# A planner that models a shared port between VectorE and GpSimd, in a fused hybrid-mixer and mixture-of-experts kernel

## The chip, the cores and the metric

The kernel runs on one core of a Trainium2 chip. A core has five engines that each work through their own instruction queue in order: TensorE (PE in the profile; its weight loads are the row PEld), VectorE (DVE), ScalarE (ACT), GpSimd (POOL) and SyncE (SP, which here issues nearly all transfers). They meet only at semaphores. The metric is the device time of one execution in microseconds (us), lower is better. Before the change the median of three runs is 1183.54 us.

## What is computed

One decoder layer over 1024 tokens of width 1024, in f32: a mixer with three kinds of causal heads, and a mixture of 32 experts of which each token uses two.

```python
h = rmsnorm(x, norm_mix) * (1.0 + scale_m) + shift_m          # scale, shift, gate from c @ w_ada
proj = h @ w_in                                               # 13 column blocks
o_ret  = retention_chunkwise(rope(rq), rope(rk), rv)          # fixed decay per head
o_hgrn = gated_linear_recurrence_chunkwise(q, k, hi, log_f)   # gate per key dimension
o_gla  = gated_linear_recurrence_chunkwise(gq, gk, gv, log_a)
merged = concat(headnorm(o_ret) * silu(rg), headnorm(o_hgrn) * silu(hg), headnorm(o_gla) * silu(gg))
x = x + gate_m * (merged @ w_out)
h = rmsnorm(x, norm_ffn) * (1.0 + scale_f) + shift_f
out = sum over the token's 2 experts of weight * ((silu(h @ w_gate[e]) * (h @ w_up[e])) @ w_down[e])
return rmsnorm(x + gate_f * out, norm_final)
```

## The kernel before

**Tiling and stages.** The tokens are eight tiles of 128, worked on in two halves of four. Each half goes through the input projection (`tok_chunk`, `t_chunk`), the retention heads (`ret_gen`), and then the gated recurrence of the HGRN2 and GLA heads together. That recurrence is the part with the most vector work: for each token tile, `hg_prep1` makes decay-weighted queries and keys at six levels (64, 32, 16, 8, 4, 2), a base level and a carried state; `hg_gen` multiplies them on TensorE, `hg_merge` writes the masked products into one score tile, `hg_dec` multiplies by the values and `hg_state` updates the carried state. Between the halves and behind the second one the output projection (`ev_out`), the second norm (`ffn_gen`) and the router (`router`) run tile by tile. Last come the 32 experts (`gate_up_gen`, `down_gen`), which stream about 100 MB of expert weights.

**Weights in two halves.** f32 weights are multiplied as two parts in the faster matmul format: `split_gen` casts a weight granule (`raw`) to a high part (`wg`, part 0) and `split_lo` subtracts that from the original to get the low part. A `raw` buffer, of which there are two, is free for the next load only when its low part is made. The normalised tokens (`HT`) are split in the same way in `spread_ev`.

**What sets the order.** The kernel is written as Python generators that a planner (`Sched`) runs when the program is built. Each engine is an `Eng` object with a planned time `free` at which its last instruction ends. Every emitted instruction goes through `Eng.__getattr__`, which prices it with `Eng.cost` and tells `Sched.note`; `note` puts its start at the later of the engine's `free` and the end of what it depends on. A generator yields until a planned time or condition, so the planned times decide in which order instructions of different generators enter each engine's queue, and when a buffer counts as free. On the chip no planned time exists: the queues run in order, and waits are semaphores.

**Choice of engine.** Two helpers choose by planned times. `av` copies on ScalarE or VectorE. `vg` takes a two-operand operation and puts it on VectorE (`V`) or GpSimd (`G`), whichever is planned to end sooner:

```python
tv = max(V.free, d) + 0.068 + 0.00104 * n + bias
tg = max(G.free, d) + 0.13 + 0.00214 * n
```

Here `n` is the number of elements per partition and `d` the time at which the inputs are there. `vg` is used for the low part of the weights (with a bias against VectorE), most of the level preparation in `hg_prep1`, the rotary sum in `ev_rope`, the gate products and head norms, the residual sum in `ev_out` and the shift in `ffn_gen`. Both engines are planned as if they never hindered each other. Nearly all rows of the profile carry line 216, the helper through which every operation is recorded, so rows are told apart by their tiles: `rx` is the recurrence's workspace, `qkc` holds queries, keys and cumulated gates, `Zh` the carried state, `om`/`oh` mixer outputs, `tmp` a scratch of 384 columns, `h`, `x` and `B` the second norm's output, input and shift.

Of the kernel before, what the change touches and what calls it, by code (L numbers as in the profile page):

```python
# [80 lines left out]
class Sched:  # L81
# [3 lines left out]
    def __init__(self):  # L85
        self.t, self.h, self.n = 0.0, [], 0
        self.base = self.end = self.last = 0.0
        self.le = None
        self.dma_free = 1.7

    def add(self, gen, delay=0.0):
        self._push(self.t + delay, gen, None)
# [38 lines left out]
    def dep(self, e):  # L131
        return self.last + (LAT if self.le is not None and self.le is not e else 0.0)

    def note(self, e, c, n=0):
        st = max(e.free, self.dep(e))
        if e.kind == "pe":
            k = int(st / WARM)
            if e.win.get(k - 1, 0.0) < 0.41 * WARM:
                c *= 2
            if n > 1:  # L140
                e.win[k] = e.win.get(k, 0.0) + min(c, (k + 1) * WARM - st)
                if st + c > (k + 1) * WARM:
                    e.win[k + 1] = st + c - (k + 1) * WARM
        e.free = self.last = st + c
        e.busy += c
        self.le = e
        self.end = max(self.end, e.free)
# [7 lines left out]
def _size(ap):  # L155
    n = 1
    for s in ap.shape[1:]:
        n *= s
    return n


class Eng:
    def __init__(self, sch, eng, kind, is_psum):
        self.sch, self.eng, self.kind, self.is_psum = sch, eng, kind, is_psum
        self.free = self.busy = 0.0
        self.win = {}
        self.table = None

# [43 lines left out]
    def __getattr__(self, name):  # L212
        f = getattr(self.eng, name)

        def call(*a, **k):
            r = f(*a, **k)  # L216
            if a:
                small = self.kind != "pe" and _size(a[0]) < 64
                self.sch.note(self, self.cost(name, a, k) + (0.12 if small else 0.0), _size(a[0]))
            return r  # L220
        return call

# [45 lines left out]
def build(tc, A, CB, CM, coff, out):  # L268
# [6 lines left out]

    V = Eng(sch, nc.vector, "dve", is_psum)
    G = Eng(sch, nc.gpsimd, "pool", is_psum)
    T_ = Eng(sch, nc.tensor, "pe", is_psum)
    SC = Eng(sch, nc.scalar, "act", is_psum)

# [13 lines left out]
    def tt(e, o, a, b, op):  # L294
        return e.tensor_tensor(o, a, b, op=op)

    def vg(o, a, b, op, bias=0.0):
        n = _size(o)
        d = sch.last + LAT
        tv = max(V.free, d) + 0.068 + 0.00104 * n + bias  # L300
        tg = max(G.free, d) + 0.13 + 0.00214 * n
        return tt(V if tv <= tg else G, o, a, b, op)

    def ts(e, o, a, s1, op0, s2=None, op1=None):
        if op1 is None:
            return e.tensor_scalar(o, a, s1, None, op0=op0)
        return e.tensor_scalar(o, a, s1, s2, op0=op0, op1=op1)
# [7 lines left out]
    def mm(o, l, r, start, stop):  # L315
        return T_.matmul(o, l, r, start=start, stop=stop, skip_group_check=True)

# [127 lines left out]
    def rstd_of(dst, ss, n, width):  # L445
        ts(G, dst, ss, 1.0 / n, OP.mult, EPS, OP.add)
        tt(G, dst, dst, epsc[:, 0:1].to_broadcast([P, width]), OP.pow)

# [4 lines left out]
    def start_gen():  # L453
# [4 lines left out]
        def wload(i):  # L458
            c = (i % 2) * D + (i // 2) * 256
            src = w_ada[:, c:c + 256].rearrange("(k p) n -> p k n", p=P)  # L460
            for h in range(2):
                ks = slice(4 * h, 4 * h + 4)
                w_at[i, h] = dma(slots[i % 4][:, ks], src[:, ks, :])
# [14 lines left out]
        wload(3)  # L478
        G.memset(epsc[:, 0:1], -0.5)
        G.memset(Zr, 0.0)  # L480
        G.memset(Zh, 0.0)
        yield (max(p_at, c_at),)
        prow = yield from mss.take()
        T_.transpose(prow[:, 0:32], rv_[0:32], ident[0:32, 0:32])
        yield None
# [104 lines left out]
    def consts_gen():  # L590
# [4 lines left out]
        prow = yield from mss.take()  # L595
        T_.transpose(prow[:, 0:NROW - 32], rv_[32:NROW], ident[32:NROW, 32:NROW])
        yield None
# [37 lines left out]
    def spread_g(g, dst_slot, src_of, scale, bias, key):  # L635
        pt = yield from mss.take()
        pv = pt.rearrange("p (k c) -> p k c", k=2)
        for kk in range(2):
            for j in range(2):
                T_.transpose(pv[:, kk, j * P:(j + 1) * P],  # L640
                             src_of(j)[:, (2 * g + kk) * P:(2 * g + kk + 1) * P], ident)
        add(spread_ev(pt, pv, g, dst_slot, scale, bias, key), max(0.0, T_.free - sch.t) + LAT)
        yield None

    def spread_ev(pt, pv, g, dst_slot, scale, bias, key):
        if key[0] == "h" and ("AB", g) not in done:
            yield lambda: ("AB", g) in done
        h32 = yield from h32s.take()
        for kk in range(2):
            k = 2 * g + kk  # L650
            if bias is None:
                act(h32[:, kk], pv[:, kk], AF.Copy, scale=scale[:, k:k + 1])
            else:
                act(h32[:, kk], pv[:, kk], AF.Identity, scale=scale[:, k:k + 1], bias=bias[:, k:k + 1])
        mss.put(pt)
        yield None
        hv = HS[dst_slot][:, 0, 2 * g:2 * g + 2]
        if key[0] == "h" and key[1] in HVG:
            av(hv, h32)
            vg(HS[dst_slot][:, 1, 2 * g:2 * g + 2], h32, hv.bitcast(F32), OP.subtract, HBIAS)  # L660
        else:
            V.tensor_copy(hv, h32)
            tt(V, HS[dst_slot][:, 1, 2 * g:2 * g + 2], h32, hv.bitcast(F32), OP.subtract)
        h32s.put(h32)
        done.add(key + (g,))
# [102 lines left out]
    def split_lo(i, w, raw, n):  # L768
        vg(w[:, 1, :, 0:n], raw[:, :, 0:n], w[:, 0, :, 0:n].bitcast(F32), OP.subtract, LO_BIAS if ("AB", 3) in done else LO_BIAS + SBIAS)
        raws.put(raw)  # L770
        w_ready[i] = (w, sch.end + LAT)
        yield 0.0
# [28 lines left out]
    def tok_chunk(first, n, groups, slots, hkey, ev, hook=None):  # L801
        for gi_, grp in enumerate(groups):
            acc = {}
            for g in range(4):
                yield from w_wait(first + g)
                for t in grp:
# [19 lines left out]
                    if g == 3:  # L826
                        add(ev(t)(p), T_.free + LAT - sch.t)
                    yield (T_.free - LEAD,)
# [55 lines left out]
    def ev_rope(t, which):  # L884
        def f(p):
            if "trig" not in done:
                yield lambda: "trig" in done
            if t >= 4 and not which:
                yield lambda: ("st", {4: 1, 5: 2, 6: 3, 7: 3}[t]) in done
            dst = RQK[:, t % 4, which, :]  # L890
            t2 = yield from t384.take()
            pv = p[:, 0:384].rearrange("p (h f) -> p h f", f=32)
            tt(V, dst.rearrange("p (h f) -> p h f", f=32), pv,
               cosT[:, t, None, :].to_broadcast([P, 12, 32]), OP.mult)
            ph = p[:, 0:384].rearrange("p (h two f) -> p h two f", two=2, f=32)
            th = t2.rearrange("p (h two f) -> p h two f", two=2, f=32)
            sb = sinT[:, t, None, :].to_broadcast([P, 6, 32])
            stt(th[:, :, 0, :], ph[:, :, 1, :], -1.0, sb, OP.mult, OP.mult)
            tt(V, th[:, :, 1, :], ph[:, :, 0, :], sb, OP.mult)
            mput(p)  # L900
            yield None
            vg(dst, dst, t2, OP.add)
            t384.put(t2)
            yield None
            d3 = dst.rearrange("p (h c) -> p h c", h=6)
            vg(d3, d3, cc("gk" if which else "gq")[:, :, None].to_broadcast([P, 6, 64]), OP.mult)
            done.add(("rope", which, t))
        return f
# [1365 lines left out]
```

## Time and profile before

| what | us |
|---|---|
| runs of the kernel before (three) | 1183.54 median, 1182.93 to 1193.45 |
| the profiled execution itself | 1184.01 |
| its span in the trace | 1182.2 |
| VectorE busy | 841.3 (71%), 1402 instructions |
| GpSimd busy | 419.9 (36%), 424 instructions |

A row of the profile names the engine, the operation, the tile that it writes and those that it reads (`out<-in`), the size as partitions x elements, and, in a list of groups, how often it occurs, its busy time, the mean duration of one, and the idle time of the engine just before such instructions. A row of the timeline gives start, duration, the instruction, and in brackets the idle time before it with what ended it. The chain of waits is followed back from the last instruction to whatever released each one. The profiled execution took 1.8 us more than its span.

### The profile page before, as it was taken

How to read it: one execution, taken by the hardware profiler on the slowest of the kernel's cores; microseconds unless marked ns; L12 is line 12 of the kernel's file. 1: busy time of each engine (PE TensorE's matmuls, PEld its weight loads, DVE VectorE, ACT ScalarE, POOL GpSimd, SP SyncE). 2: the span in 40 equal slices, each digit the busy share in tenths (PEclk: the TensorE clock that was granted, in tenths of full speed). 3: DMA queues.
4: the chain of work that ended last, by engine and by line, in shares of the span. 5: the costliest groups of instructions: out<-in, count | busy, mean ns of one | idle time of the engine just before them, and what ended most of it. 6: DMA issues, size and time to landing. Idle time of an engine off the chain costs nothing.

```text
span 1182.2 us, 17072 instructions
## 1 busy us (share of the span) xinstructions
PE 1042.8 (88%) x6168; PEld 853.1 (72%) x6168; DVE 841.3 (71%) x1402; ACT 520.3 (44%) x974; POOL 419.9 (36%) x424
## 2 busy tenths in 40 slices
PE   3889999888989889997899999849999898899995
PEld 2889998787878788897888888736566555455654
DVE  6685767988897754448798976658666666565767
ACT  4513334455543423345455545336445444344544
POOL 4452232445633422104463413351322323332225
PEclk9889999799999999998899989859999999999997
DMA  9475556111213522233421158865999999999976
GB/s 313 140 213 185 163 167 219 41 54 31 96 54 123 172 77 58 60 92 111 137 77 41 41 177 308 302 216 155 303 295 311 302 318 307 294 315 318 329 232 261
DMA packets 96039, 218.99 MB, mean 185 GB/s; under 512 B 13342, under 2 KB 56538, under 8 KB 95954
## 3 DMA queue, kind: packets, MB, share of 16 engines
q1 hardware_dynamic: 89010, 201.67, 51.5%
q0 software_dynamic: 6944, 16.22, 6.1%
q8 instruction: 50, 0.82, 0.3%
q14 instruction: 35, 0.29, 0.1%
HBM read 201.64 MB, written 24.38 MB: 191 GB/s over the span
## 4 chain that ended last, share of the span: by engine, by line
PE 38%; DMA 25%; DVE 21%; issue 6%; ACT 4%; POOL 4%; SPq 0%; DVEq 0%; POOLq 0%; ACTq 0%; another core or an unknown queue 0%
PE mm L216 25%; DMA HG<-expert_w_up 10%; PE lv L216 10%; DVE rx L216 5%; PE ms L216 4%; DMA gu<-expert_w_up 4%; DMA dn<-expert_w_down 3%; DVE qkc L216 3%; DMA dg<-expert_w_down 3%; DMA h<-w_ada 2%; DVE HT L216 2%; DVE wg L216 2%; DMA raw<-w_in 2%; DVE h L216 1%; DVE tmp L216 1%
## 5 line engine op out<-in xcount | busy, mean ns | idle before, releaser
L216 PE MATMUL mm<-wg,HT 128*128 128x384 f32 (+2 forms) x1920 | 365.5, 343 | 24.3 <-DVE tmp L216 14.2
L216 PEld LDWEIGHTS mm<-wg,HT 128*128 128x128 f32 x1920 | 322.5, 199 | 36.6 <-issue 12.3
L216 PE MATMUL mm<-ew,xT 128*96 128x512 f32 x576 | 166.9, 428 | 10.2 <-DVE ew L216 8.0
L216 ACT ACTIVATE wg<-raw 128x768 fp32r<-128x768 f32 (+2 forms) x115 | 89.3, 779 | 124.3 <-PE mm L216 73.9
L216 PEld LDWEIGHTS mm<-ew,xT 128*96 128x96 f32 x576 | 92.4, 167 | 63.1 <-issue 15.2
L216 POOL TENSOR_TENSOR wg<-raw,wg 128x768 fp32r<-128x768 f32 (+1 forms) x36 | 69.8, 1942 | 188.8 <-ACT wg L216 119.6
L216 DVE TENSOR_TENSOR wg<-raw,wg 128x768 fp32r<-128x768 f32 (+2 forms) x90 | 83.6, 930 | 65.3 <-ACT wg L216 64.6
L216 PE MATMUL lv<-rx 64*128 64x64 f32 (+5 forms) x1216 | 104.8, 287 | 18.3 <-DVE rx L216 14.0
L216 POOL DMA_INDIRECT x2d<-y,tki x30 | 60.1, 2004 | 166.5 <-DVE y L216 74.9
L216 PEld LDWEIGHTS lv<-rx 64*128 64x128 f32 (+2 forms) x1216 | 92.9, 192 | 35.8 <-issue 22.6
L216 DVE TENSOR_TENSOR ew<-HG,ew 128x1024 fp32r<-128x1024 f32 x68 | 81.7, 1219 | 33.7 <-ACT ew L216 33.7
L216 PE MATMUL mm<-HT,wg 128*128 128x256 f32 (+1 forms) x576 | 97.6, 324 | 0.1
L216 ACT ACTIVATE rx<-rx 128x64 f32<-128x64 f32 (+4 forms) x180 | 68.6, 417 | 52.1 <-DVE rx L216 30.2
L216 ACT ACTIVATE ew<-HG 128x1024 fp32r<-128x1024 f32 x66 | 68.3, 1052 | 50.9 <-DMA HG<-expert_w_up 45.0
L216 PEld LDWEIGHTS mm<-HT,wg 128*128 128x128 f32 x576 | 82.3, 190 | 9.0 <-issue 1.0
L216 POOL DMA_INDIRECT xg<-h2d,tki x32 | 43.5, 1359 | 94.6 <-PE ms L216 74.6
L216 DVE SCALAR_TENSOR_TENSOR y<-lv,lists,GF 96x512 f32<-96x512 f32 x64 | 45.0, 741 | 44.1 <-PE lv L216 44.1
L216 PE MATMUL mm<-ewx,xT 128*96 128x512 f32 x192 | 60.7, 449 | 5.3 <-DVE ewx L216 4.5
L216 PE MATMUL lv<-dn,hT 128*96 128x512 f32 x128 | 60.8, 597 | 1.7 <-ACT hT L216 1.7
L216 PE MATMUL lv<-dg,hT 128*96 128x512 f32 x128 | 60.0, 594 | 2.3 <-ACT hT L216 2.3
L216 DVE TENSOR_TENSOR rx<-rx,qkc 128x320 f32<-128x320 f32 (+4 forms) x94 | 58.6, 652 | 1.1 <-ACT rx L216 1.0
L216 POOL TENSOR_TENSOR rx<-qkc 128x512 f32<-128x512 f32 (+2 forms) x34 | 36.0, 1066 | 45.4 <-PE lv L216 40.6
(307 smaller groups left out, 1706.3 us busy)
## 6 DMA issues: line engine op xcount, KB each, us to landing
raw<-w_in SPq DMA_DIRECT2D x64, 384.0 KB
HG<-expert_w_gate SPq DMA_DIRECT2D x46, 512.0 KB
HG<-expert_w_up SPq DMA_DIRECT2D x46, 512.0 KB
h<-w_ada SPq DMA_DIRECT2D x32, 512.0 KB
dn<-expert_w_down SPq DMA_DIRECT2D x32, 512.0 KB
dg<-expert_w_down SPq DMA_DIRECT2D x32, 512.0 KB
raw<-w_out SPq DMA_DIRECT2D x26, 384.0 KB
gu<-expert_w_gate SPq DMA_DIRECT2D x18, 512.0 KB
```

The lines of the kernel that those rows point to most:

```text
L216: r = f(*a, **k)
```

## The change

`Eng` gets two new fields: `held`, the planned end of the last operation of this engine that uses a port common to VectorE and GpSimd, and `other`, which links the two engines. An operation on one of them counts as using the port when it writes at least 64 elements per partition, is no memset, and either has more than one SBUF operand or touches no PSUM at all. `note` then starts it no sooner than the other engine's `held`, and sets its own. `vg` adds the other engine's `held` to both estimates. No operation is added or removed, and no other rule of the planner is touched.

```diff
-    def note(self, e, c, n=0):
+    def note(self, e, c, n=0, port=None):
         st = max(e.free, self.dep(e))
+        if port is not None:
+            st = max(st, port.held)
+            e.held = st + c
...
-        self.free = self.busy = 0.0
+        self.free = self.busy = self.held = 0.0
+        self.other = None
...
                 small = self.kind != "pe" and _size(a[0]) < 64
-                self.sch.note(self, self.cost(name, a, k) + (0.12 if small else 0.0), _size(a[0]))
+                port = None
+                if self.other is not None and _size(a[0]) >= 64 and name != "memset" and (
+                        sum(hasattr(x, "shape") and not self.is_psum(x) and _size(x) > 1 for x in a[1:]) > 1
+                        or not any(self.is_psum(x) for x in a if hasattr(x, "shape"))):
+                    port = self.other
+                self.sch.note(self, self.cost(name, a, k) + (0.12 if small else 0.0), _size(a[0]), port)
...
+    V.other, G.other = G, V
...
-        tv = max(V.free, d) + 0.068 + 0.00104 * n + bias
-        tg = max(G.free, d) + 0.13 + 0.00214 * n
+        tv = max(V.free, d, G.held) + 0.068 + 0.00104 * n + bias
+        tg = max(G.free, d, V.held) + 0.13 + 0.00214 * n
```

The program that comes out has 347 instructions in GpSimd's order where there were 441, and 1511 in VectorE's where there were 1426; ScalarE's go from 941 to 950. By kind, what left GpSimd are 19 low parts of weights (13 of 768 columns, 6 of 512), 9 level subtractions `rx<-qkc` of 512 columns, some 20 level products `rx<-rx,qkc`, and gate products, head norms, residual sums and shifts. All engines' orders are rearranged around that. The helper's line number becomes 220.

GpSimd's queue at the last output projection, ahead of the router: `om`, `x` and `h` with numbers are the residual and the second norm of tiles 4 and 5, `rs` the norm's factor, `wg` a weight's low part. Before:

```order
L216 TENSOR_TENSOR wg_6553<-raw_6462,wg_6553 128x2x256
L216 TENSOR_TENSOR om_6483<-om_6483,tmp_6693 128x256
L216 TENSOR_TENSOR x_6493<-x_6493,tmp_6706 128x256
L216 TENSOR_SCALAR rs_6726<-ss_6725 128x1
L216 TENSOR_TENSOR rs_6726<-rs_6726,epsc 128x1
L216 TENSOR_SCALAR rs_6740<-ss_6739 128x1
L216 TENSOR_TENSOR rs_6740<-rs_6740,epsc 128x1
L216 TENSOR_TENSOR om_6487<-om_6487,B_126 128x512
L216 TENSOR_TENSOR h_6497<-h_6497,B_126 128x512
L216 TENSOR_TENSOR wg_6779<-raw_6683,wg_6779 128x768
L216 TENSOR_SCALAR r_gm<-r_m_6789 128x1
```

And after, on the same engine at the same place:

```order
L220 TENSOR_TENSOR wg_6384<-raw_6301,wg_6384 128x768
L220 TENSOR_SCALAR rsh<-ssh 128x10
L220 TENSOR_TENSOR rsh<-rsh,epsc 128x10
L220 TENSOR_SCALAR rs_6726<-ss_6725 128x1
L220 TENSOR_TENSOR rs_6726<-rs_6726,epsc 128x1
L220 TENSOR_SCALAR rs_6749<-ss_6748 128x1
L220 TENSOR_TENSOR rs_6749<-rs_6749,epsc 128x1
L220 TENSOR_SCALAR r_gm<-r_m_6779 128x1
```

The two residual sums, the two shifts and the low parts have left GpSimd's queue here; only the norm factors and the router's small operations stay.

VectorE's queue in the recurrence of the first half, from the head norm (`ssh`) of its first tile to the first update of the carried state `Zh`. Before:

```order
L216 CAST wg_2236<-raw_2044 128x768
L216 TENSOR_REDUCE ssh<-lv_2227 128x6
L216 TENSOR_REDUCE ssh<-lv_2227 128x4
L216 TENSOR_TENSOR rx<-qkc 128x512
L216 TENSOR_TENSOR Zh<-Zh,rx 128x384
L216 TENSOR_TENSOR Zh<-Zh,rx 128x256
L216 TENSOR_TENSOR rx<-qkc 128x512
L216 TENSOR_TENSOR rx<-rx,qkc 128x16x16
L216 TENSOR_TENSOR rx<-rx,qkc 128x20x16
L216 CAST wg_2286<-raw_2220 128x768
L216 TENSOR_TENSOR rx<-rx,qkc 128x32x8
L216 TENSOR_TENSOR rx<-rx,qkc 128x40x8
```

And after, on the same engine at the same place:

```order
L220 TENSOR_TENSOR wg_2214<-raw_2065,wg_2214 128x768
L220 TENSOR_REDUCE ssh<-lv_2238 128x6
L220 TENSOR_REDUCE ssh<-lv_2238 128x4
L220 TENSOR_TENSOR Zh<-Zh,rx 128x384
L220 TENSOR_TENSOR Zh<-Zh,rx 128x256
L220 TENSOR_TENSOR wg_2266<-raw_2219,wg_2266 128x768
L220 TENSOR_TENSOR Zh<-Zh,lv_2251 64x3x64 x2
L220 TENSOR_TENSOR Zh<-Zh,lv_2251 32x64 x4
L220 TENSOR_TENSOR rx<-qkc 128x512 x2
L220 TENSOR_TENSOR rx<-rx,qkc 128x16x16
L220 TENSOR_TENSOR rx<-rx,qkc 128x20x16
```

The two casts of high parts have gone to ScalarE and two low parts have come from GpSimd, and the state update stands ahead of the next tile's level work instead of behind it.

## The prediction

> **What bounds the kernel now.** I read the page's busy shares and its chain of waits first, then the stages, then VectorE and GpSimd side by side, then their groups.
>
> ```profile
> PE 1042.8 (88%) x6168; PEld 853.1 (72%) x6168; DVE 841.3 (71%) x1402; ACT 520.3 (44%) x974; POOL 419.9 (36%) x424
> PE 38%; DMA 25%; DVE 21%; issue 6%; ACT 4%; POOL 4%; SPq 0%; DVEq 0%; POOLq 0%; ACTq 0%; another core or an unknown queue 0%
> ```
>
> TensorE leads the chain, VectorE has a fifth of it, GpSimd a twenty-fifth. The stages differ (columns: stretch in us, its length, busy time and count of PE, PEld, DVE, ACT, POOL, granted clock, DMA share, GB/s):
>
> ```profile
> 0.00:95.00 95.00, 66.58 (x325) 63.20 (x326) 69.56 (x145) 36.33 (x57) 45.76 (x52) 0.91 0.69 220
> 95.00:207.00 112.00, 108.66 (x836) 101.40 (x834) 75.16 (x92) 41.22 (x67) 27.81 (x22) 1.00 0.58 182
> 207.00:390.00 183.00, 161.00 (x1206) 147.07 (x1206) 156.54 (x267) 88.55 (x203) 83.99 (x74) 0.94 0.22 69
> 390.00:532.00 142.00, 133.61 (x838) 120.75 (x837) 79.56 (x155) 51.08 (x94) 34.15 (x45) 0.99 0.32 90
> 532.00:715.00 183.00, 166.31 (x1226) 153.24 (x1226) 155.00 (x293) 92.61 (x216) 80.39 (x90) 0.92 0.33 106
> 715.00:787.00 72.00, 51.46 (x337) 48.73 (x336) 45.46 (x140) 26.73 (x63) 29.89 (x57) 0.82 0.78 270
> 787.00:1182.00 395.00, 355.14 (x1412) 218.73 (x1412) 260.05 (x314) 183.73 (x277) 117.89 (x87) 0.96 0.89 287
> ```
>
> The third and fifth rows are the two recurrences; the second and fourth are mostly projections, with TensorE at 97% and 94%. TensorE is busy 88% and 91% there, VectorE 86% and 85%: they pace each other, and TensorE's idle 22.0 and 16.7 us bound what faster vector work can win. The last row, the experts, has DMA at 0.89 and hardly an operation that the planner may move; I expect it to shift as a block.
>
> Now the two engines at one place of the first recurrence, VectorE first:
>
> ```profile
> 249.17 0.68 DVE L216 TENSOR_TENSOR rx<-qkc 128x512 f32<-128x512 f32 x1
> 249.77 0.81 DVE L216 TENSOR_TENSOR rx<-rx,qkc 128x256 f32<-128x256 f32 x2
> 250.98 3.29 DVE L216 TENSOR_TENSOR rx<-rx,qkc 128x256 f32<-128x256 f32 x2
> ```
>
> ```profile
> 248.59 2.51 POOL L216 TENSOR_TENSOR rsh<-rsh,epsc 128x10 f32<-128x10 f32 x1
> 250.69 1.27 POOL L216 TENSOR_TENSOR rx<-qkc 128x512 f32<-128x512 f32 x1
> 251.92 2.00 POOL L216 TENSOR_TENSOR wg<-raw,wg 128x768 fp32r<-128x768 f32 x1
> ```
>
> The same pair of level products takes 0.81 us and, beside two large GpSimd operations, 3.29. Lost: 2.48 us of 3.27 us of GpSimd time, 0.76 per us. The small power `rsh` beside the first two rows costs them nothing. So the port that the change models exists, and only GpSimd's large operations hold it. The Trainium skill's page "SBUF — State Buffer" (Who interferes with whom) says that a VectorE instruction with two SBUF inputs and a GpSimd one that reads SBUF exclude each other, the later waiting for the other's end; the pair at 250.98 agrees, the power does not.
>
> How much of this there is, by VectorE's groups (busy, mean ns of one), with an undisturbed row for their forms, the last of them with the shortest of the scans as first of three durations:
>
> ```profile
> L216 DVE TENSOR_TENSOR wg<-raw,wg 128x768 fp32r<-128x768 f32 x61 | 62.2, 1021 | 41.9 <-ACT wg L216 41.6
> L216 DVE TENSOR_TENSOR rx<-qkc 128x512 f32<-128x512 f32 x32 | 27.4, 862 | 1.9 <-PE lv L216 1.8
> L216 DVE TENSOR_TENSOR rx<-rx,qkc 128x320 f32<-128x320 f32 x42 | 25.9, 620 | 0.5 <-ACT rx L216 0.5
> L216 DVE TENSOR_TENSOR HT<-h,HT 128x512 fp32r<-128x512 f32 x24 | 24.8, 1032 | 5.2 <-ACT HT L216 4.5
> L216 DVE TENSOR_TENSOR_SCAN qkc<-cst,qkc 128x128 f32<-128x128 f32 x32 | 23.1, 784 | 0.1
> L216 DVE SCALAR_TENSOR_TENSOR h<-x,rs,A 128x512 f32<-128x512 f32 x12 | 17.4, 1452 | 1.4 <-POOL rs L216 1.4
> L216 DVE TENSOR_TENSOR rx<-rx,qkc 128x256 f32<-128x256 f32 x25 | 13.5, 540 | 0.5 <-ACT rx L216 0.5
> ...
> 726.89 0.95 DVE L216 TENSOR_TENSOR wg<-rw,wg 128x768 fp32r<-128x768 f32 x1
> 218.66 0.47 DVE L216 TENSOR_TENSOR rx<-rx,qkc 128x320 f32<-128x320 f32 x1
> 325.72 0.69 DVE L216 TENSOR_TENSOR HT<-h,HT 128x512 fp32r<-128x512 f32 x1
> 730.80 0.75 DVE L216 SCALAR_TENSOR_TENSOR om<-om,rs,A 128x512 f32<-128x512 f32 x1 [0.22 <-POOL rs L216]
> L216 DVE TENSOR_TENSOR_SCAN qkc<-cst,qkc x32: 391/418/2027, 207.4 to 546.9; 128x128 f32<-128x128 f32 x32
> ```
>
> Mean less undisturbed, times count: wg 4.3, rx 512 5.8, rx 320 6.3, HT 8.2, scans 12.6, h 8.4, rx 256 3.4 (at half of 0.81): 49.0 us lost in seven groups.
>
> **The change, part by part.** Nothing is computed less; operations change engine. GpSimd's groups before:
>
> ```profile
> L216 POOL TENSOR_TENSOR wg<-raw,wg 128x768 fp32r<-128x768 f32 x29 | 58.9, 2033 | 122.9 <-DVE wg L216 67.9 <-ACT wg L216 53.7 <-DMA h<-w_ada 0.7
> L216 POOL TENSOR_TENSOR rx<-qkc 128x512 f32<-128x512 f32 x24 | 29.1, 1218 | 42.8 <-PE lv L216 38.3 <-DVE qkc L216 4.5
> L216 POOL TENSOR_TENSOR rx<-rx,qkc 128x256 f32<-128x256 f32 x23 | 21.3, 929 | 18.2 <-ACT rx L216 18.2
> L216 POOL TENSOR_TENSOR rx<-rx,tmp 128x384 f32<-128x384 f32 x10 | 13.8, 1384 | 20.7 <-DVE tmp L216 18.2 <-DVE r_ne L216 1.8 <-DVE r_m L216 0.7
> L216 POOL TENSOR_TENSOR wg<-raw,wg 128x512 fp32r<-128x512 f32 x7 | 10.9, 1565 | 65.9 <-ACT wg L216 65.9
> L216 POOL TENSOR_TENSOR om<-om,tmp 128x384 f32<-128x384 f32 x8 | 8.9, 1116 | 13.8 <-DVE tmp L216 13.8
> L216 POOL TENSOR_TENSOR h<-h,B 128x512 f32<-128x512 f32 x5 | 8.0, 1599 | 3.6 <-DVE h L216 3.6
> ```
>
> *The exchange.* By the orders, these leave GpSimd for VectorE: 13 wg of 768 columns, 9 rx of 512, 14 rx of 256, 7 rx of 384, 6 wg of 512, 7 om, 4 h. Off GpSimd: 26.4 + 11.0 + 13.0 + 9.7 + 9.4 + 7.8 + 6.4 = 83.7 us. Onto VectorE, at 0.95, 0.68, 0.41, 0.55, 0.69, 0.55, 0.69 (0.55 lies between the rows for 320 and 512 columns): 12.4 + 6.1 + 5.7 + 3.9 + 4.1 + 3.9 + 2.8 = 38.9 us. So VectorE wins only if each us that GpSimd holds the port costs it more than 38.9 / 83.7 = 0.46 us. These are 60 of the 94 that GpSimd's order has less; the rest have the same sizes or smaller ones, and I let them trade alike, so that GpSimd loses some 110 us in all and VectorE gains some 50 of its own work. A further gain or loss lies in where the moved operation stands: on GpSimd it ran beside VectorE and had a short queue; on VectorE it ends in half the time once it starts, but starts behind all that VectorE was given before it.
>
> *What a held us costs.* From below: the seven VectorE groups lose 49.0 us against 150.9 us of the seven GpSimd groups, 0.32. From above: the pair's 0.76. I take 0.4: it is a mean that is wanted, so the group figure is nearer, raised because VectorE's smaller groups also lose. Both ends stay for the range. At 0.4 VectorE gets back 33.5 of its 38.9 us: nearly an even trade.
>
> *The recurrences.* From the first scan of a half to its fourth state update VectorE's order grows by 25 and 33 instructions. They are nearly all of the forms without wg: 41 such moved ones take 47.9 us off GpSimd and put 22.4 on VectorE, 1.17 and 0.55 each. So +13.8 and +18.2 on VectorE, 29.3 and 38.6 off GpSimd, at 0.4 giving back 11.7 and 15.4: +2.1 and +2.8, about +5. With VectorE at 85% I charge all of it to the path; whatever waits next is TensorE for `rx`. Queued behind a moved operation are the masked writes of the scores and the state update, and TensorE's next level or value product waits for those.
>
> *The output projections and the second norm.* Here the path runs through these operations:
>
> ```profile
> PE mm L216 <- DVE tmp L216: 18.7, 11, 4.4
> PE ms L216 <- POOL x L216: 2.5, 1, 2.5
> 727.06 1.38 POOL om L216
> 728.45 1.41 POOL x L216
> ```
>
> The 18.7 us of TensorE wait on a product that stands in VectorE's queue behind the `h` operations, which are stretched from 0.75 to 1.45. Four of five `h<-h,B` leave GpSimd, so I strike four fifths of their 8.4 us, -6.7, and add 4 x 0.69 = 2.8. The two residual sums of 256 columns in the chain cost 2.79 us on GpSimd and some 0.42 each on VectorE: -1.9. Sum -6.
>
> *Weights.* A low part that ends sooner frees `raw` sooner, and the chain runs through that:
>
> ```profile
> 159.08 1.31 POOL wg L216
> 160.40 4.96 DMA raw<-w_in
> ```
>
> The 512-column low parts of this stage leave GpSimd and take 0.69 us in place of 1.31, two such places in the chain, and about 0.9 more for a 768-column one: -2. The price is a longer line on VectorE: before its 61 wg of 768 columns it sits idle 41.9 us, 0.69 each, for ScalarE's cast, so 19 more bring some 13 us in which what stands behind them waits too. In the projections its idle 36.8 and 62.4 us cover that. In the recurrences the cover is thin; what falls there I leave to the lower end of the exchange.
>
> *The start.* Three `HT` low parts move to VectorE in front of its matrix-vector sums: +2.1, against about as much lost now to the same operations on GpSimd. Zero, with +-3 for the range. On SyncE's queue two raw loads move ahead of the mask's load, and the mask is needed only in the recurrence, over 100 us later.
>
> *The experts.* Their order holds the same instructions, and the transfers at 0.89 cover them. Zero; if a buffer freed elsewhere let the expert loads begin at another time, that is the last row's 395 us moving, which I count as wrong below.
>
> Sum: +5 - 6 - 2 = -3, and -4 with the two casts of 768 columns that go from VectorE to ScalarE, whose 88.6 and 92.6 busy us of 183 cover them. The profiled execution took 1184.0 (0.5 over the median): **1180 us**, its own range 1172 to 1190.
>
> **Rivals.** *The block is nearly whole.* The mechanism of the pair at 250.98, everywhere: VectorE's next two-operand operation waits until GpSimd's has ended. At 0.76 the recurrences get back 51.6 for 32.0: -20, and with the other two terms 1184 - 28 = 1156. It fits inside TensorE's 38.7 idle us. For it: scans and HT take twice and one and a half times their undisturbed rows. Against it: the groups' mean is under half of the pair's, since much of the time VectorE has something to do, or to wait for, that the port doesn't touch. By the rule of the Trainium skill's page named above, one us lost for each held, the recurrences would win 35.9 and the sum would be an estimated 1140; the group means don't agree with it as an average.
>
> *VectorE's queue becomes the bound.* Place: the two recurrences. The moved operations cost 32.0 us, but what stretches VectorE is mostly the GpSimd work that stays (18 low parts and 15 of 24 level subtractions), so little comes back. At 0.1 per us 6.8 comes back: +25 - 8, 1201. It ends over 1% slower once the exchange pays under 0.18. For it: VectorE at 85% while GpSimd stands at 45%, and the planner now charges GpSimd for VectorE's whole planned queue. Against it: the 0.32.
>
> *It doesn't do what it says:* the orders change, but the loss just moves to other pairs: 1184.
>
> **How the numbers follow.** Forecast 0.40, whole block 0.27, VectorE bound 0.25, nothing 0.08. Within 1% (about what a measurement of this kernel can tell from no change) means 1171.7 to 1195.4. Faster: 0.27 and 0.04 of the forecast's low end, 0.31. Slower: 0.25. Same: 0.44. The range 1157 to 1203 leaves out half of the whole-block case and a quarter of the VectorE case, 0.20.
>
> **What would show it.** Right: the groups' means on VectorE fall toward 0.68, 0.95, 0.41 with about half of the excess gone; VectorE's busy time stays within 15 us of 841; GpSimd's falls by about 100; TensorE's wait for `tmp` falls by 4 to 8; the recurrences last 183 +-6 each. Wrong: a recurrence that shrinks by 10 (whole block) or grows by 10 with PE waiting for `rx` (VectorE bound), or a change in the experts' 395 us.

## The result and the profile after

| kernel | runs | median us | range |
|---|---|---|---|
| before, on the same chip | 4 | 1184.97 | 1182.93 to 1193.45 |
| after | 4 | 1144.2 | 1140.45 to 1150.52 |

The ratio is 0.967, with a 95% interval of 0.963 to 0.971: the change takes 3.3% off, some 40 us where 4 were forecast, and lies below the forecast's range. The profiled execution has a span of 1141.4 us, 40.8 less than the one before.

First the busy shares of the changed kernel and its chain of waits:

```profile
PE 1023.4 (90%) x6168; PEld 837.4 (73%) x6168; DVE 827.6 (73%) x1487; ACT 521.6 (46%) x983; POOL 298.4 (26%) x330
DMA 26%; PE 5%; POOL 1%; DVE 1%; ACT 1%; issue 0%; SPq 0%; DVEq 0%; POOLq 0%; another core or an unknown queue 0%; ACTq 0%
```

GpSimd gave up 121.5 us of work, and yet VectorE, with 85 instructions more, is 13.7 us less busy. The chain's shares add up to a third of the span: in this profile it could be followed back only through the experts, so it says nothing of the stages in front of them.

Those are compared by landmarks instead, since a stretch of fixed times holds different work in the two kernels. Here are the landmarks on VectorE's timeline, in the kernel before (start, duration, instruction: first gate sum of the first half, its fourth update of the carried state, and the same two of the second half), and on GpSimd's the first gather of the experts:

```profile
207.40 0.74 DVE L216 TENSOR_TENSOR_SCAN qkc<-cst,qkc 128x128 f32<-128x128 f32 x2
...
365.89 0.91 DVE L216 TENSOR_TENSOR Zh<-Zh,lv 32x64 f32<-32x64 f32 x4
...
532.14 1.96 DVE L216 TENSOR_TENSOR_SCAN qkc<-cst,qkc 128x128 f32<-128x128 f32 x1
...
692.93 0.46 DVE L216 TENSOR_TENSOR Zh<-Zh,lv 32x64 f32<-32x64 f32 x2
...
778.73 1.24 POOL L216 DMA_INDIRECT xg<-h2d,tki  x1 [2.04 <-DVE cnt L216]
```

The same five in the changed kernel:

```profile
202.02 0.73 DVE L220 TENSOR_TENSOR_SCAN qkc<-cst,qkc 128x128 f32<-128x128 f32 x2
...
349.83 0.91 DVE L220 TENSOR_TENSOR Zh<-Zh,lv 32x64 f32<-32x64 f32 x4
...
512.23 1.05 DVE L220 TENSOR_TENSOR_SCAN qkc<-cst,qkc 128x128 f32<-128x128 f32 x3
...
665.12 0.46 DVE L220 TENSOR_TENSOR Zh<-Zh,lv 32x64 f32<-32x64 f32 x2
...
740.97 1.25 POOL L220 DMA_INDIRECT xg<-h2d,tki  x1 [1.00 <-DVE ctr L220]
```

| from, to | before | after | difference |
|---|---|---|---|
| start, first gate sum | 207.4 | 202.0 | -5.4 |
| recurrence of the first half | 158.5 | 147.8 | -10.7 |
| its end, second half's gate sum | 166.2 | 162.4 | -3.8 |
| recurrence of the second half | 160.8 | 152.9 | -7.9 |
| its end, first gather | 85.8 | 75.9 | -9.9 |
| first gather, end | 403.5 | 400.4 | -3.0 |

The two recurrences give 18.6 us, and the last output projection with the second norm and the router 9.9. The experts hardly move.

Busy time by stage of the changed kernel, in stretches cut at about these landmarks (columns as in the prediction's table):

```profile
95.00:202.00 107.00, 104.27 (x819) 98.52 (x818) 74.56 (x99) 39.63 (x65) 14.98 (x13) 1.00 0.61 186
202.00:366.00 164.00, 151.91 (x1146) 140.00 (x1146) 142.81 (x285) 85.91 (x196) 45.89 (x42) 0.94 0.24 72
512.00:680.00 168.00, 158.14 (x1239) 147.00 (x1238) 147.27 (x320) 92.30 (x219) 49.73 (x60) 0.98 0.38 117
680.00:741.00 61.00, 46.26 (x318) 43.66 (x316) 43.87 (x146) 25.23 (x60) 16.52 (x49) 0.90 0.86 309
```

The recurrences in the kernel before, cut at the same places of the program:

```profile
207.00:382.00 175.00, 153.00 (x1151) 139.68 (x1151) 151.51 (x257) 84.00 (x192) 82.60 (x73) 0.94 0.21 66
532.00:708.00 176.00, 159.51 (x1188) 146.99 (x1188) 149.55 (x284) 88.09 (x206) 79.52 (x89) 0.91 0.31 97
```

TensorE's busy time there is nearly the same (153.0 and 151.9; 159.5 and 158.1). What went is its idle time: from 22.0 us to 12.1 and from 16.5 to 9.9. VectorE has 28 and 36 instructions more in these two stretches and is 8.7 and 2.3 us less busy.

VectorE's groups after, the seven that the prediction added up:

```profile
L220 DVE TENSOR_TENSOR wg<-raw,wg 128x768 fp32r<-128x768 f32 x75 | 71.4, 953 | 29.8 <-ACT wg L220 29.6
L220 DVE TENSOR_TENSOR rx<-qkc 128x512 f32<-128x512 f32 x41 | 28.2, 708 | 1.3 <-PE lv L220 1.2
L220 DVE TENSOR_TENSOR rx<-rx,qkc 128x320 f32<-128x320 f32 x48 | 24.3, 506 | 0.0
L220 DVE TENSOR_TENSOR HT<-h,HT 128x512 fp32r<-128x512 f32 x27 | 22.5, 833 | 2.0 <-ACT HT L220 1.3
L220 DVE TENSOR_TENSOR rx<-rx,qkc 128x256 f32<-128x256 f32 x39 | 19.2, 493 | 0.0
L220 DVE TENSOR_TENSOR_SCAN qkc<-cst,qkc 128x128 f32<-128x128 f32 x32 | 12.3, 447 | 0.0
L220 DVE SCALAR_TENSOR_TENSOR h<-x,rs,A 128x512 f32<-128x512 f32 x12 | 8.9, 746 | 0.5 <-POOL rs L220 0.3
```

And what is left of GpSimd's large groups:

```profile
L220 POOL TENSOR_TENSOR wg<-raw,wg 128x768 fp32r<-128x768 f32 x17 | 33.7, 1985 | 52.9 <-DVE wg L220 26.5 <-ACT wg L220 26.3
L220 POOL TENSOR_TENSOR rx<-qkc 128x512 f32<-128x512 f32 x15 | 17.3, 1158 | 62.4 <-PE lv L220 62.4
L220 POOL TENSOR_TENSOR rx<-rx,qkc 128x256 f32<-128x256 f32 x9 | 10.0, 1113 | 123.1 <-ACT rx L220 123.0
```

Against the undisturbed rows of the prediction (0.95, 0.68, 0.47, 0.69, 0.405, 0.391, 0.75) the seven VectorE groups now lose 0.2 + 1.1 + 1.7 + 3.9 + 3.4 + 1.8 + 0 = 12 us, where they lost 49.0: 37 came back. The three GpSimd groups fell from 109.3 us to 61.0.

TensorE's waits after, in total us, times, longest:

```profile
PE lv L220 <- DVE qkc L220: 13.7, 4, 6.2
PE mm L220 <- DVE tmp L220: 10.8, 7, 3.4
PE mm L220 <- DVE om L220: 9.1, 7, 4.0
...
PE lv L220 <- DVE rx L220: 3.6, 4, 2.1
...
PE ms L220 <- DVE x L220: 2.0, 3, 0.9
```

And three rows of the kernel before that the prediction had not shown:

```profile
PE lv L216 <- DVE rx L216: 14.0, 10, 3.5
...
PE ms L216 <- DVE x L216: 6.1, 3, 3.2
...
PE mm L216 <- DVE om L216: 2.3, 4, 1.3
```

The wait for `tmp` fell by 7.9, but 6.8 of it came up again as a longer wait for `om`. The waits for `rx`, which belong to the recurrences, fell by 10.4; that for `x`, the residual ahead of the second norm, by 4.1, and that of 2.5 for GpSimd's `x` is gone. All but the last of these are waits for results of VectorE, in both kernels.

TensorE's weight loads wait for GpSimd as well. The largest two such rows before, and the largest one after:

```profile
PEld lv L216 <- POOL rx L216: 4.9, 2, 3.6
PEld ms L216 <- POOL x L216: 3.2, 2, 2.7
...
PEld lv L220 <- POOL HT L220: 1.1, 1, 1.1
```

All rows of this kind add up to 13.6 us before and 1.3 after. ScalarE's waits for GpSimd's `rx` fell from 21.3 to 10.5 us.

### The profile page after: what moved, and what is told of

Read it like the earlier page. It is cut to its first block, busy times and chain, and to the rows that moved or that the text cites. A ratio compares the mean times of both kernels' runs of the same rounds, so it can differ in the third digit from the quotient of the medians.

```text
span 1141.4 us, 17029 instructions
## 1 busy us (share of the span) xinstructions
PE 1023.4 (90%) x6168; PEld 837.4 (73%) x6168; DVE 827.6 (73%) x1487; ACT 521.6 (46%) x983; POOL 298.4 (26%) x330
## 5 line engine op out<-in xcount | busy, mean ns | idle before, releaser
L220 PE MATMUL mm<-wg,HT 128*128 128x384 f32 (+2 forms) x1920 | 355.9, 337 | 24.0 <-DVE om L220 9.1
L220 PEld LDWEIGHTS mm<-wg,HT 128*128 128x128 f32 x1920 | 314.5, 195 | 35.5 <-issue 12.8
L220 PE MATMUL mm<-ew,xT 128*96 128x512 f32 x576 | 171.5, 435 | 11.0 <-DVE ew L220 7.8
L220 ACT ACTIVATE wg<-raw 128x768 fp32r<-128x768 f32 (+2 forms) x118 | 92.3, 783 | 125.4 <-PE mm L220 76.0
L220 DVE TENSOR_TENSOR wg<-raw,wg 128x768 fp32r<-128x768 f32 (+2 forms) x111 | 97.0, 875 | 51.2 <-ACT wg L220 50.6
L220 DVE TENSOR_TENSOR rx<-rx,qkc 128x320 f32<-128x320 f32 (+4 forms) x117 | 61.9, 563 | 0.1
L220 POOL DMA_INDIRECT xg<-h2d,tki x32 | 36.5, 1140 | 91.1 <-PE ms L220 80.1
L220 PE MATMUL mm<-ewx,xT 128*96 128x512 f32 x192 | 57.2, 432 | 3.1 <-DVE ewx L220 2.5
L220 DVE COPY_PREDICATED rx<-msk,lv 128x320 f32<-128x320 uint8 (+1 forms) x80 | 47.5, 655 | 4.3 <-PE lv L220 4.0
L220 PEld LDWEIGHTS ms<-cst,xg 96*128 96x128 f32 x256 | 34.3, 202 | 20.7 <-issue 12.5
```

## The experiments

Two questions had to be told apart. The first: the change does two things at once, it puts operations on other engines and it gives every large operation a later planned time, which reorders all queues. Theory A: the engines bring the gain. Theory B: the order does. The second, once A stood: what about the engines pays, the port that GpSimd no longer holds, or something else. All intervals are 95%. The ratios compare with runs of the kernel before on the same chip, whose medians lay between 1181.66 and 1183.47 us; differences from the changed kernel use its 1144.2 from another chip.

### Engines or order

The engine of each of the 496 calls of `vg` was written down for both kernels: 163 on GpSimd before, 69 after; 123 went to VectorE, 30 to GpSimd, and one call of each kernel has no counterpart in the other. First, the planner of the kernel before with each call forced to the engine of the changed kernel:

```diff
     def vg(o, a, b, op, bias=0.0):
+        key = vg_key()
+        if key in ON_G or key in ON_V:
+            return tt(G if key in ON_G else V, o, a, b, op)
         n = _size(o)
```

> The planner of before, without the port in its times, but every two-operand operation stands on the engine that the changed kernel gives it. Theory A (the engines: a microsecond that GpSimd holds the port costs VectorE more than the 0.46 us at which the trade is even): at least two thirds of the 41 us come, 1145 to 1158. Theory B (the order: the queues now stand in an order that agrees with what the chip does): under a third comes, 1172 to 1186. If both are needed, in between.

Measured: 1153.55 us, ratio 0.975 (0.969 to 0.981): 30 of the 41 us.

The reverse, the changed planner with the same lines and the tables of the kernel before:

> The planner of the changed kernel with the port in its times, but every two-operand operation stands on the engine it had before. Theory A: within 10 us of before, 1175 to 1190. Theory B: at least two thirds of the 41 us, 1145 to 1158.

Measured: 1181.34, ratio 1.000 (0.996 to 1.003). Theory B falls: the port in the planned times, by itself, is worth nothing in total. It does move time between the stages: by the landmarks its recurrences last 170 and 171 us, 21 more than before, and the other stretches 22 less. So the table by stages above shows where the queues' new order put the gain, and is no price of each stage's change. Then the changed kernel without the port in the planned times, where only the choice sees it:

```diff
-            st = max(st, port.held)
             e.held = st + c
```

> The engine choice sees the other engine's hold, but planned starts are not delayed by it: half of the change. Theory A: close to the changed kernel if about as many operations leave GpSimd (168 two-operand operations of any size stay there against 150, and 241 before): 1148 to 1162. Theory B: most of the gain is missing, 1170 to 1186.

Measured: 1141.12, ratio 0.963 (0.957 to 0.969), better than either theory had it and no worse than the whole change. And the changed kernel with everything on VectorE:

```diff
-        return tt(V if tv <= tg else G, o, a, b, op)
+        return tt(V, o, a, b, op)
```

> The changed kernel with every operation of the choice on VectorE, so that GpSimd keeps only its fixed work. In the changed kernel its large two-operand operations still hold the port for 97 us, beside which VectorE loses 28 us, 0.29 per us: under the even price of 0.46. Theory A in the form of that price: VectorE gains about 45 us of work and loses 28 us of stretch, so slower than the changed kernel by 5 to 20 us, 1150 to 1165. Rival (any held us costs more than it is worth, through the waits behind it): faster than the changed kernel, under 1140.

Measured: 1161.54, ratio 0.979 (0.974 to 0.985). The last GpSimd operations are worth keeping there: moving them as well costs 17 us against the changed kernel. By the landmarks its recurrences last 166.2 and 160.9 us, 26 more than in the changed kernel, and the other stretches 8 less. So theory A holds as far as the engines go, and moving everything is too much. Its reason, that a held us costs more than 0.46, is taken up below. The 11 us between the forced engines and the whole change are not explained by any run.

### Which operations, and how many

The forced tables again, once for the recurrence alone (`hg_prep1` and `hg_state` as after, the rest as before), once the other way round:

> The planner of before; only the two-operand operations of the recurrences (level preparation and state decay) stand on the changed kernel's engines, all others on their old ones. If the gain of 30 us that the choice alone brought comes from the recurrences, where GpSimd's large operations are thickest: 18 to 28 us of it, 1155 to 1166. If it comes from the second norm, the residual sums and the weights' low parts: under 10 us, 1174 to 1186.

Measured: 1161.58, ratio 0.981 (0.976 to 0.986).

> The complement: the recurrences keep their old engines, and low parts of weights, rotary sums, head norms, gate products, residual sums and shifts stand where the changed kernel has them. Gain from the recurrences: 1170 to 1186. Gain from the rest: 1155 to 1166. The two parts together should give about the 30 us of the choice alone if they add.

Measured: 1150.69, ratio 0.973 (0.968 to 0.978), below both ranges. The two gains, 22 and 33 us, add up to more than the 30 of both together, so they are not separate terms. By the landmarks the recurrences last 148.6 and 154.5 us in this second kernel, nearly as short as in the changed one, though their own operations stay where they were: moving what runs beside them, the weights' low parts among it, was enough there.

A charge that knows nothing of the port, on the kernel before:

```diff
-        tg = max(G.free, d) + 0.13 + 0.00214 * n
+        tg = max(G.free, d) + 0.13 + 0.00214 * n + 1.6
```

> The kernel before with one number added: GpSimd is charged 1.6 us more in each choice, and nothing models a port. 144 two-operand operations of any size stay on GpSimd, against 150 in the changed kernel and 241 before. If it is enough that fewer operations stand on GpSimd: at least two thirds of the gain, 1140 to 1156. If it must be those that meet VectorE's own port operations: half or less, 1163 to 1182.

Measured: 1154.86, ratio 0.979 (0.972 to 0.986). By the traces that leaves 151 `TENSOR_TENSOR` on GpSimd, where the changed kernel has 156 and the one before 250. Some two thirds of the gain come without any model of the port. The busy shares of this kernel, and then of the one with everything on VectorE:

```profile
PE 1034.6 (90%) x6168; PEld 843.8 (73%) x6168; DVE 845.1 (73%) x1496; ACT 520.2 (45%) x979; POOL 299.0 (26%) x325
PE 1037.2 (89%) x6168; PEld 852.7 (74%) x6168; DVE 836.6 (72%) x1554; ACT 523.9 (45%) x985; POOL 217.5 (19%) x261
```

With the flat charge GpSimd is as free as in the changed kernel, and VectorE is 3.8 us busier than before.

### What a held us and a VectorE us cost

Three kernels add work that nobody reads at each of the 64 level steps of the recurrences, outside the planner, so that the order of the rest stays as it is. `junk` is a scratch tile and `cst` a constant:

```diff
     def hg_prep1(it, sl):
         t, w = it
+        for _ in range(2):
+            nc.gpsimd.tensor_tensor(junk, cst[:, 0:256], cst[:, 0:256], op=OP.add)
```

> The changed kernel with two more additions of 256 columns on GpSimd at each of the 64 level steps of the recurrences, from a constant into a scratch tile that nobody reads: 128 operations of about 0.6 us, 77 us in which GpSimd reads SBUF, not known to the planner; the queues of the other engines are the same. If holding the port is what costs VectorE: 0.3 to 0.76 us per us, 20 to 50 us slower than the changed kernel, 1164 to 1194. If the gain was shorter waits for GpSimd's own results and the hold is small change: under 12 us, 1140 to 1156.

Measured: 1165.22, ratio 0.985 (0.979 to 0.992): 21 us more than the changed kernel, for 96.7 us of such additions.

With four `nc.gpsimd.memset(junk, 0.0)` in place of the two additions:

> The same places, with four memsets of 256 columns each in place of the two additions: about as much more GpSimd time (256 of about 0.3 us), but nothing is read. It delays GpSimd's own results as much as the additions do, without holding the port for reads. If the port costs: under 12 us, 1140 to 1156, and clearly less than the additions. If GpSimd's queue and its late results cost: about the same as the additions.

Measured: 1140.08, ratio 0.962 (0.958 to 0.967). 82.3 us on GpSimd that read nothing cost nothing.

With the two additions on VectorE (`nc.vector`):

> The changed kernel with two more additions of 256 columns at each of the 64 level steps, this time on VectorE and not known to the planner: 128 operations of about 0.41 us, 52 us of VectorE work that nobody needs. The additions on GpSimd stretched VectorE by 28 us and cost 21 to 25 us, 0.8 per us. If VectorE's time is one thing to the path, whether it is work or waiting: 0.8 x 52 = 42, 1175 to 1195. If added work hides in VectorE's idle time and only waiting for the port costs: under 15 us, 1142 to 1159. The second would explain alone why 44 us of moved work cost nothing.

Measured: 1193.43, ratio 1.011 (1.007 to 1.015): 49 us more than the changed kernel.

Their busy shares, one line each, of the additions on GpSimd:

```profile
PE 1034.2 (89%) x6168; PEld 847.0 (73%) x6168; DVE 855.8 (74%) x1487; ACT 523.4 (45%) x983; POOL 407.1 (35%) x458
```

of the memsets:

```profile
PE 1028.1 (90%) x6168; PEld 841.9 (74%) x6168; DVE 826.0 (72%) x1487; ACT 522.1 (46%) x983; POOL 382.5 (33%) x586
```

of the additions on VectorE:

```profile
PE 1033.3 (87%) x6168; PEld 844.9 (71%) x6168; DVE 884.7 (75%) x1615; ACT 524.0 (44%) x983; POOL 309.0 (26%) x330
```

In the first, VectorE executes the same 1487 instructions as the changed kernel in 28.2 us more: 0.29 per us held. The memsets leave it at 826.0. The additions on GpSimd took 0.76 us each, where 0.6 was expected.

The same three in the kernel before:

> The kernel before with four memsets of 256 columns on GpSimd at each level step, as in the changed kernel's test: 77 to 80 us more of GpSimd time without reads, queues of the other engines as before. If the kernel before waited for GpSimd's late results, so that part of the gain is their shorter way: 10 to 40 us slower than before, 1194 to 1225. If GpSimd's lateness never mattered: within 8 us, 1176 to 1192.

Measured: 1193.55, ratio 1.012 (1.004 to 1.020): 12 us (5 to 24 by the interval) for 80.2 us of memsets that cost nothing in the changed kernel. VectorE is not busier for it:

```profile
PE 1046.8 (88%) x6168; PEld 856.9 (72%) x6168; DVE 838.5 (71%) x1402; ACT 518.2 (44%) x974; POOL 493.1 (41%) x680
```

> The kernel before, with two additions of 256 columns from a constant into a scratch tile that nobody reads, on GpSimd at each of the 64 level steps of the recurrences: the same work that held the port for 97 us and cost 21 to 25 us in the changed kernel. The same GpSimd time without reads cost the kernel before some 10 us. If a held us costs the kernel before no more than the changed one (0.22 to 0.25): 1205 to 1217, the port alone then explains about 30 of the change's 40 us, to be set against the moved work. If it costs more where GpSimd is fuller (0.4 and up): 1225 to 1240, and the port is most of the gain.

Measured: 1216.83, ratio 1.030 (1.026 to 1.034), at the upper edge of the first case: 33.6 us, of which the memsets' row puts 11.9 on GpSimd's time alone. VectorE lost 25.9 us (its row is below) to 103.1 us of additions: 0.25 per us held.

> The kernel before, with the same two additions on VectorE at the same places, some 60 us of work that nobody reads. In the changed kernel it cost 45 to 49 us. If VectorE is as much the path in the kernel before: 1228 to 1235, and the 44 us of moved work cost the change some 35 us. If GpSimd's late results give VectorE slack in the kernel before, so that moved work is cheap: 1195 to 1215, and the exchange needs no further cause.

Measured: 1225.63, ratio 1.037 (1.033 to 1.041): a little under the first case. VectorE's time in the recurrences is as dear in the kernel before as in the changed one.

Where the memsets' 12 us go is seen in the weights that TensorE loads for the level products (idle time in front of them, and what ended it). In the kernel before:

```profile
L216 PEld LDWEIGHTS lv<-rx 64*128 64x128 f32 (+2 forms) x1216 | 92.9, 192 | 35.8 <-issue 22.6 <-POOL rx L216 4.9 <-ACT wg L216 2.2
```

with the memsets:

```profile
L216 PEld LDWEIGHTS lv<-rx 64*128 64x128 f32 (+2 forms) x1216 | 95.3, 197 | 43.9 <-POOL rx L216 20.3 <-issue 16.5 <-POOL junk L1081 3.0
```

and in the changed kernel:

```profile
L220 PEld LDWEIGHTS lv<-rx 64*128 64x128 f32 (+2 forms) x1216 | 90.4, 186 | 19.5 <-issue 15.8 <-ACT rx L220 0.9 <-DVE rx L220 0.3
```

In the kernel before, TensorE already waited for level products of GpSimd, and 80 us of memsets on GpSimd make it wait longer: 4.9 us became 20.3, while the idle time in front of these loads grew by 8.1 in all. In the changed kernel that releaser is not among those shown.

### The moved results, with the port held as before

The last experiment takes the first one (engines as after, planner as before, 1153.55) and leaves the time of what moved on GpSimd:

```diff
+        if key in MOVED:
+            for _ in range(-(-_size(o) // 256)):
+                nc.gpsimd.tensor_tensor(junk, cst[:, 0:256], cst[:, 0:256], op=OP.add)
         if key in ON_G or key in ON_V:
```

> The kernel before with the operations put on the engines of the changed kernel (1153.6 us alone), and for each of 119 operations that moved to VectorE its time left on GpSimd as well: additions of 256 columns from a constant into a scratch tile, as many as its columns need, which nobody reads. So the results come from VectorE while GpSimd holds the port about as long as before. If all of the gain is the port: slower than before by the moved work, 1205 to 1230. If the results' coming sooner and without GpSimd's queue is half of the gain: 1180 to 1195. If the port matters little: 1160 to 1175.

Measured: 1195.45, ratio 1.012 (1.008 to 1.016), just above the upper edge of the middle case. The additions came to 194.7 us, more than the 121 that the change takes off GpSimd. Its busy shares:

```profile
PE 1051.4 (88%) x6168; PEld 859.4 (72%) x6168; DVE 888.0 (74%) x1487; ACT 523.8 (44%) x983; POOL 493.0 (41%) x561
```

and those of the first experiment, without the additions:

```profile
PE 1029.5 (90%) x6168; PEld 840.5 (73%) x6168; DVE 831.0 (72%) x1487; ACT 522.8 (46%) x983; POOL 301.1 (26%) x330
```

TensorE's wait for VectorE's `rx` in the first experiment, and then in this one:

```profile
PE lv L320 <- DVE rx L320: 4.0, 5, 1.7
...
PE lv L347 <- DVE rx L347: 11.4, 11, 2.7
```

The operations stand on the same engines and in the same order in both, so most of the shorter wait for `rx` (14.0 before, 3.6 in the changed kernel) goes with how much GpSimd works beside VectorE, and not with where the results are made.

The busy shares of the kernel before with the additions on VectorE, and then with those on GpSimd, complete the table below:

```profile
PE 1055.0 (87%) x6168; PEld 863.8 (71%) x6168; DVE 893.2 (73%) x1530; ACT 521.4 (43%) x974; POOL 421.1 (35%) x424
```

```profile
PE 1055.9 (87%) x6168; PEld 862.7 (71%) x6168; DVE 867.2 (72%) x1402; ACT 518.6 (43%) x974; POOL 522.5 (43%) x552
```

| from, to | VectorE busy, us | time, us | time per VectorE us |
|---|---|---|---|
| before, additions on VectorE | +51.9 | +42.4 | 0.82 |
| after, additions on VectorE | +57.1 | +49 | 0.86 |
| after, additions on GpSimd | +28.2 | +21 | 0.74 |
| engines alone, additions for the moved | +57.0 | +41.9 | 0.74 |
| before, additions on GpSimd (less the memsets' 11.9) | +25.9 | +21.7 | 0.84 |
| before, after | -13.7 | -40.8 | 3.0 |
| before, engines alone | -10.3 | -29.9 | 2.9 |
| before, engines and additions for the moved | +46.7 | +12.2 | 0.3 |

(Busy time from the profiled executions; time from the medians of kernel and kernel before, or of the two kernels, within some 5 us.)

The first five rows change no operation's engine. They agree on a rate: a us of VectorE's time, whether work or waiting for the port, costs 0.74 to 0.86 us. (In the fourth, what GpSimd's lateness costs is not taken off, so its rate is rather too high.) The last three change engines, and all three lie below that rate by about the same amount. At 0.8, VectorE explains -11, -8 and +37 us; the rest is -30, -22 and -25. The flat charge, with VectorE 3.8 us busier and 27 us gained, leaves -30.

So an estimated 22 to 30 us of the gain are not VectorE's time. What these kernels have in common is that results are made on VectorE that GpSimd made before, in an order that the planner then chose anew. It isn't a gain for every result: from the changed kernel to the one with everything on VectorE, VectorE is 9.0 us busier, 7 at the rate, and the time is 17 us longer, so there the rest is +10. And four of the five rows with the rate add their work in the recurrences alone; for the other stages it is carried over, not measured.

## Why the prediction was wrong

*What a held us costs: too low for what the change took off.* 0.4 was taken, from bounds of 0.32 and 0.76. The seven VectorE groups got back 37 us, and by the named counts 83.7 us went off GpSimd: 0.44. VectorE's whole busy time says more. It fell by 13.7 us, although the prediction let some 50 us of work move onto it; so an estimated 64 us came back for 121.5 off GpSimd, 0.52. In the recurrences the prediction put 32.0 on VectorE and 11.0 less was measured, which makes an estimated 43 us back for 66.5 off GpSimd, 0.65. Yet additions put on GpSimd in the same place cost VectorE only 0.25 and 0.29. Why taking work off gives back more than adding it costs was not tested; one number doesn't serve for both.

*The exchange: forecast as even, measured as a gain.* 38.9 us were put on and 33.5 forecast to come back, "nearly an even trade", and the recurrences were to make VectorE 5 us busier. They made it 11.0 less busy, and the whole kernel 13.7; that lies inside the 15 that were named as the sign, but on the winning side. At 0.8 it is worth 11 us of time where the sum had a small loss. This term was mis-sized, and by itself it would not have been enough.

*Where the moved operation stands: the step that failed most.* The prediction named it ("A further gain or loss lies in where the moved operation stands"), and then gave it no term in the sum. In the recurrences it wrote "With VectorE at 85% I charge all of it to the path", so the only thing that could come out there was VectorE's balance, +5. Measured, -10.7 and -7.9, with TensorE's busy time nearly unchanged. In the whole kernel the rows that don't rest on the complete change, the forced engines without and with the additions, put 22 and 25 us on something other than VectorE's time. With VectorE's -11 they make -33 to -36, most of the 40.8. What that something is, is shown only in part. A result of GpSimd took 0.93 to 2.03 us by the rows of the prediction and stood in a queue that waits for the operand of whatever is first in it (122.9 us ahead of the low parts of 768 columns alone); the same result takes 0.41 to 0.95 on VectorE. The waits for GpSimd fell, those of TensorE's weight loads from 13.6 to 1.3 us; that would be about half of the 22 to 25 if every us of it counted.

*The output projections and the second norm: right in kind, too small.* `h` fell to its undisturbed 0.75 us and the wait for `tmp` by 7.9, as forecast (4 to 8). The stage behind the second recurrence alone gave 9.9 where -6 was set for all of them, though the new order alone shortens it as much (75.3 us in the changed planner with the engines of before, against 75.9). Part of the wait came back as the one for `om`.

*Weights, start, experts.* The stretch to the first gate sum gave 5.4 where -2 and 0 +-3 stood, the part between the recurrences 3.8; the experts 3.0 of 403, as good as nothing, as forecast.

*The rivals.* "The block is nearly whole" gave 1156 and named a recurrence 10 us shorter as its sign. The sign came. VectorE's own balance there, -11.0, lies past the middle between the forecast's +5 and this rival's -20, and the estimated 0.65 that came back per us is nearer to its 0.76 than to 0.4; the additions, at 0.25 and 0.29, speak against it. So it was right about the direction, and no run settles its size. "VectorE's queue becomes the bound" fell, though where nothing is left on GpSimd the trade does turn, by 17 us. "It doesn't do what it says" fell as well, with one remark: what the words put first, the port in the planned times, is worth nothing here; the port in the choice of engine does the work, and a flat charge does two thirds of it.

What stays open: how the 22 to 30 us divide between the shorter operation, GpSimd's queue, and the order that the planner makes of the new engines. The memsets show that lateness on GpSimd costs the kernel before and not the changed one; they don't give the shares. Nor was a kernel tried that moves single operations by who waits for them. TensorE's busy time is also 19.4 us lower for the same 6168 instructions, at a mean granted clock of 0.964 against 0.944. That doesn't decide the result: the kernel that drops the port from the planned times was as fast with TensorE busy for 1034.2 us, and the forced engines with the additions leave their 25 us with TensorE 8.6 us busier than before.

## What to carry to other kernels

When work moves between two engines, the balance of their busy times is one term; what else follows from the new place, such as who waits for each moved result and in which order the queues then stand, is another, and here it was the larger by estimate (22 to 30 us against 11). Look at the consumer's wait rows before setting it to nothing, and don't expect them to give all of it. Where a planner overuses a slow engine, measure a flat charge first: it shows how much of the gain needs a model at all.

## What the runs showed of the hardware

GpSimd additions with two operands in SBUF slow VectorE, and far from one for one: 96.7 us of them cost VectorE 28.2 us in the changed kernel, 103.1 us cost 25.9 in the one before, and 82.3 us of memsets none. The Trainium skill's page "SBUF — State Buffer" (Who interferes with whom) says that a VectorE instruction with two SBUF inputs contends with a GpSimd one that reads SBUF, not with one that only writes it; the memsets agree. It calls the shared ports an exclusive lock; the single pair that lost 0.76 per us of GpSimd's time comes near to that. As a mean the loss was only 0.25 to 0.29 per us of added work; why it is so far below one was not measured. A large GpSimd operation with a single SBUF operand was not tried.

Adding 80 us to the least busy of the four computing engines, GpSimd at 36%, cost the kernel before 12 us without VectorE being any busier. In this kernel an engine that is two thirds idle is on the path through the lateness of some of its results: TensorE's weight loads waited 20.3 us for them instead of 4.9.
